# A hybrid decoder layer: the first operands of the feed-forward's down stage are read back inside the last slab, the slab order is swapped, and two products share one PSUM bank

## The chip, the core and the metric

The kernel runs on one core of a Trainium2 chip. TensorE (PE) multiplies out of SBUF into eight PSUM banks; VectorE (DVE), ScalarE (ACT) and GpSimd (POOL) do the elementwise work; SyncE (SP) issues nearly all DMAs, in order, from one queue. The metric is the device time of one execution in microseconds (us): the median of three runs of the kernel before is 1153.75 us (1151.14 to 1154.53).

## The reference

One layer over 1024 prompt tokens and 8 sequences of 4 sample tokens, 1056 tokens in all, at model width 1024 and feed-forward width 2816, in float32. The change touches the second half of it:

```python
    mix = jnp.concatenate([a, m], axis=-1) @ w_out
    x = x + _rms(mix, n_mix_post)
    f = _rms(x, n_ffn_pre)
    f = (jax.nn.silu(f @ w_gate) * (f @ w_up)) @ w_down
    x = x + _rms(f, n_ffn_post)
    x = x + jax.nn.sigmoid(x @ w_ple_gate) * (p @ w_ple)
```

`_rms` is a root-mean-square norm over the 1024 channels. What comes before it (the input projection, windowed attention with sinks, the pooling mixer) is left as it was.

## The kernel before

**Number format.** Every float32 operand is split into a high part `h` and a low part `l` (a cast on ACT, L167, then a subtraction on DVE, L168), and each product is three matmuls, hh, hl and lh, accumulated in one bank. All matmuls are issued by line L126, so PE's rows in the profile are told apart by their operands: `fh`/`fl` are feed-forward inputs, `wh`/`wl` weights, `sh`/`sl` sums of weights, `hid` the hidden activations, `qh`/`ql` quarters of the down weights and `xo` hidden operands read back from DRAM.

**Tiling.** The tokens form three groups of 352. The feed-forward has 22 pairs of column tiles (below: pairs c = 0 to 21), taken in 11 slabs of two. Group 2 is multiplied directly: 24 matmuls for the gate, 24 for the up projection, and 48 for the part of the down projection that belongs to a slab. Groups 0 and 1 together go through a Strassen-Winograd scheme: with two halves of the weights and the two groups as a 2x2 block matrix, seven products of 12 matmuls each replace eight. The products of a pair are P1 (operand B11), P2 (B21), S2, S3, P4 (T4), S1 and S4; S products take their weights from `w_sums` (L1096), which makes four sums of 128x512 on POOL (L1106) in place over the raw weights, and splits the results on ACT and DVE.

**The walk.** `WALK` lists (slab, groups) in order: first five slabs for group 2 alone (`FIRST2`: 2, 4, 6, 8, 10), then all eleven slabs, those of `FIRST2` with groups (0, 1) and the others with (0, 1, 2). The program therefore ends its walk with slab 10 for groups 0 and 1. A pair of (0, 1, 2) holds 7x12 + 48 = 132 matmuls; a pair of (0, 1) holds 84, and the first pair of a (0, 1) slab another 48, the group-2 down products (`downs`, L1337) of the slab before it. `gate_up` (L1122) takes the products of one pair in order; the order of the matmuls is the order of the program text. ACT copies P1 out of its bank (L1145), DVE adds P2 to the copy, and ACT applies Silu to the sum (L1152).

**Hidden operands.** `stage` (L1060) splits each of the seven hidden operands of a pair into an `st` tile and, when a set of two slabs is full, issues its store to DRAM (L1070, `xd<-st`). The last set, set 5, holds one slab alone. `down7` (L1234) runs the down stage of groups 0 and 1 in steps; `x_get` (L1222) issues the loads of a step's operands (`xo<-xd`). `q_sum` (L308, the POOL instruction in L316) makes sums of quarters of the down weights on POOL.

**Around them.** `turn` counts matmuls, and a `chain(steps, wait)` is a list of small steps (the norms of a group, `ple_steps`, L1309) that starts only when `wait` more matmuls were issued; the first of its matmuls takes `acc`, the sum of squares that DVE accumulates in L874. `need` (L318) prepares weights four items ahead. The order of ACT, DVE, POOL and SP instructions is chosen by a scheduler when the program is built; each engine then runs its list in order. The last stage (`ple_first`, `ple_rest`) repeats the scheme for the per-layer gate.

Of the kernel before, what the change touches and what calls it, by code (L numbers as in the profile page):

```python
# [10 lines left out]
F32 = mybir.dt.float32  # L11
F32R = mybir.dt.float32r
AF = mybir.ActivationFunctionType
ALU = mybir.AluOpType
# [47 lines left out]
def trunk_kernel(  # L62
# [43 lines left out]
    def nm(s):  # L106
        cnt[0] += 1
        return f"{s}{cnt[0]}"
# [113 lines left out]
    def direct_item(src, shape):  # L222
        return item("direct", add_plan(src, shape))

    WGU, WD = [], []
    for s, gs in WALK:
        pairs_of = []
        for i in range(SLAB):
            c = SLAB * s + i
            jg = direct_item(w_gu[c, 0], [P, KC, P])  # L230
            if 0 not in gs:
                ju = direct_item(w_gu[c, 1], [P, KC, P])
            if i == 0 and WD and 2 in WALK[len(WD) - 1][1]:
                last_s = WALK[len(WD) - 1][0]
                WD[-1] = [direct_item(w_dn[last_s, j], [P, SLAB, 512]) for j in range(2)]
            if 0 in gs:
# [4 lines left out]
        WD.append(None)  # L241


    SETS = [list(range(i, min(i + 2, NSLAB))) for i in range(0, NSLAB, 2)]
# [3 lines left out]
    STEPS = [(k, (0, 1)) for k in FIVE + TWO]  # L248
    STEPS += [(k, at) for at in ((2, 3), (4, 5)) for k in FIVE]
    STEPS += [(k, (2, 3, 4, 5)) for k in TWO]  # L250
    WDN = {}
    for k, at in STEPS:
        for e in at:
# [54 lines left out]
    def q_sum(k, e):  # L308

        out, a, b, op = {  # L310
            "S1": ("22", "21", "22", ALU.add),
            "S3": ("21", "11", "21", ALU.subtract),
            "S2": ("11", "22", "11", ALU.subtract),
            "S4": ("12", "12", "11", ALU.subtract),
        }[k]
        ge.tensor_tensor(q_load(out, e), q_load(a, e), q_load(b, e), op=op)  # L316

    def need(k, ahead=LOOK):  # L318

        for i in range(len(made), min(k + ahead + 1, len(ITEMS))):  # L320
            kind, js = ITEMS[i]
            if kind in ("direct", "home"):
                w_split(js[0], act_tile if kind == "home" else None)
                made[i] = pairs[js[0]]
            elif kind == "half":
                w_load(js[0])
                t = w_tile([P, KC, P], "w2")
                made[i] = t[:, 0:4, :], t[:, 4:8, :]
                split(*made[i], raws[js[0]][:, 4:8, :])
            elif kind == "quarter":  # L330
                made[i] = q_split(q_load(QUARTER[js[0]], js[1]))
                for n in {"P4": ("S1", "S3", "S2"), "P2": ("S4",)}.get(js[0], ()):
                    for e in js[2]:
                        q_sum(n, e)
            elif kind == "dsum":
                out = {"S1": "22", "S3": "21", "S2": "11", "S4": "12"}[js[0]]
                made[i] = q_split(q_load(out, js[1]))
            else:
                for j in js:
                    w_load(j)  # L340
                made[i] = w_sums(*(raws[j] for j in js))
            for kind, js in ITEMS[i + 1 : i + 3]:
                if kind not in ("quarter", "dsum"):
                    for j in js:
                        w_load(j)
            for kind, js in ITEMS[i + 1 : i + 7]:
                if kind in ("quarter", "dsum"):
                    q_loads(kind, js)
        return made[k]

    def gemm(ps, ops, start=True, stop=True):

        last = len(ops) - 1
        for i, (wh, wl, xh, xl) in enumerate(ops):
            mm(ps, wh, xh, start=start and i == 0, stop=False)
            mm(ps, wh, xl, start=False, stop=False)
            mm(ps, wl, xh, start=False, stop=stop and i == last)

    def ops8(w, xs):

# [699 lines left out]
    def stage(key, pair, src):  # L1060

        e = next(i for i, ps in enumerate(SETS) if pair in ps)
        i = SETS[e].index(pair)
        if (key, e) not in staged:
            staged[key, e] = act_tile([P, 2, 2, N], F32R, "st")
        t = staged[key, e]
        split(t[:, 0, i, :], t[:, 1, i, :], src)
        if i == len(SETS[e]) - 1:
            d = dpool.tile([P, 2, 2, N], F32, name=nm("xd"))
            nc.sync.dma_start(d[:, :, : i + 1], t[:, :, : i + 1].bitcast(F32))  # L1070
            spilled[key, e] = d

    evens = []

# [47 lines left out]
    def gate_up(items, pair, slot, gs, pending):  # L1122

        ig, iu, is_ = items
        n = N

        def product(w, x):
            ps = bank()
            gemm(ps[:, :n], ops4(w, x))
            turn(12)  # L1130
            return ps[:, :n]

        def direct(w):
            ps = bank()
            gemm(ps[:, :n], ops8(w, fs[2]))
            turn(24)
            return ps[:, :n]

        def add(out, a, ps):
            ve.tensor_tensor(out, a, ps, op=ALU.add)  # L1140

        wg = need(ig)
        if 0 in gs:
            p1 = tmp(n, "p1")
            se.copy(p1, product(quarter(wg, 0), f7["B11"]))  # L1145
# [7 lines left out]
        if pending and 0 in gs:  # L1153
# [4 lines left out]
        if 2 in gs:  # L1158
            if slot == 0:
                new_hid[0] = half(2, F32R, "hid")  # L1160
            hid_put(slot, sl)
        if pending and 0 not in gs:
            pending()
        if 0 not in gs:
            return
        if 2 not in gs:
            p4 = product(quarter(wu, 1), f7["T4"])
# [12 lines left out]
        add(p1, p1, product(s["S4"], f7["B22"]))  # L1180
        se.activation(p1, p1, AF.Silu)
        ve.tensor_tensor(u3, u3, p1, op=ALU.mult)
        pair_put(pair, slot, c21, u3)
# [222 lines left out]
    def ple_first(a):  # L1406

        wp, w = W1[a]
        need(wp)
        wg = need(w)  # L1410
        if not p1s:
            p1s.append(half(0, s="p1"))
        p1 = p1s[0][:, a // 2, :]
        se.copy(p1, product(quarter(wg, 0), e7["B11"]))
        c11 = tmp(N, "c11")
        ve.tensor_tensor(c11, p1, product(quarter(wg, 1), e7["B21"]), op=ALU.add)
        ple_end(c11, wp, a, 0)

    def ple_rest(a, b):
        wp, w, js = W2[a]  # L1420
# [37 lines left out]
    for a in (7, 5, 3, 1):  # L1458
        ple_first(a)
    for m in range(4):  # L1460
        embed_early(W1[1][0], m, 1)
    finish(list(chains))
    for a, b in PAIRS:
        ple_rest(a, b)
# [86 lines left out]
```

## Time and profile before

| | before |
|---|---|
| median of three runs | 1153.75 us |
| profiled execution | 1154.42 us |
| its span in the trace | 1152.6 us |
| VectorE busy | 858.1 us (74%), 1303 instructions |
| ScalarE busy | 508.9 us (44%), 919 instructions |
| GpSimd busy | 266.2 us (23%), 193 instructions |

The span is the stretch that the trace covers; 1.8 us of the execution lie outside it. The five slabs of group 2 alone, then the eleven others, fill the trace up to 840 us; the down stage of groups 0 and 1 starts at 866 us, and the per-layer stage fills the last 120 us. A row of a view names line, engine, operation and tiles, and gives starts and durations in us; a wait is put down to the producer that came last.

### The profile page before, as it was taken

Reading aid. Unit: us, or ns where it says so; the run is one execution under the profiler, and the core shown is the slowest. Engines: PE = TensorE matmul, PEld = TensorE weight load, DVE = VectorE, ACT = ScalarE, POOL = GpSimd, SP = SyncE. Lnnn points to the kernel's source line nnn. Section 1 sums busy time; section 2 is a strip of 40 time slices with the busy share of each in tenths; the row PEclk is TensorE's granted clock in tenths of the full one; section 3 lists DMA queues with packets and bytes.
Section 4 is the critical chain, followed back from the end, with each engine's and each line's share of the span. In section 5 each row is a group of like instructions: output and inputs, shape, how many; then the busy total and the mean of one; then the engine's idle time right before and its main releaser. Section 6 shows DMA issues by size and latency. Waiting matters only on the chain.

```text
span 1152.6 us, 17678 instructions
## 1 busy us (share of the span) xinstructions
PE 1092.3 (95%) x6867; PEld 1070.8 (93%) x6867; DVE 858.1 (74%) x1303; ACT 508.9 (44%) x919; POOL 266.2 (23%) x193
## 2 busy tenths in 40 slices
PE   8999999999999999999999999999819999789997
PEld 8999988899999999999999999999719999789996
DVE  6766379768979758686876976876875387898877
ACT  7322377645654333434433343433615522454442
POOL 0054022100000212232231321331251086000231
PEclk9999999999999999999999999999869999899998
DMA  7121311623633212532613523527539656725242
GB/s 280 55 68 55 99 48 38 243 87 113 244 128 129 74 44 67 188 134 79 225 59 122 199 73 107 188 82 274 191 107 406 235 192 213 269 69 188 101 128 76
DMA packets 54451, 163.60 MB, mean 142 GB/s; under 512 B 5828, under 2 KB 20068, under 8 KB 54368
## 3 DMA queue, kind: packets, MB, share of 16 engines
q1 hardware_dynamic: 53040, 160.70, 39.6%
q10 hardware_dynamic: 1328, 1.77, 0.5%
q8 instruction: 54, 0.88, 0.3%
q14 instruction: 29, 0.24, 0.1%
HBM read 124.59 MB, written 37.86 MB: 141 GB/s over the span
## 4 chain that ended last, share of the span: by engine, by line
PE 72%; DVE 11%; DMA 5%; ACT 4%; POOL 4%; issue 3%; POOLq 0%; SPq 0%; ACTq 0%; DVEq 0%
PE b L126 71%; POOL wr L1106 4%; DMA wr<-in_w_gu_dram 2%; DVE st L168 2%; DVE u L1270 2%; DVE wl L168 1%; ACT wh L167 1%; DVE ql L168 1%; DVE sl L168 1%; DMA xr<-in_x_dram 1%; ACT sh L167 1%; PE b L120 1%; DVE acc L874 1%; ACT h L454 1%; DMA xo<-xd 0%
## 5 line engine op out<-in xcount | busy, mean ns | idle before, releaser
L126 PE MATMUL b<-fh,wh 128*128 128x352 f32 x712 | 230.1, 323 | 0.3 <-DVE o L1202 0.3
L126 PE MATMUL b<-fh,wl 128*128 128x352 f32 x712 | 228.8, 321 | 0.0
L126 PE MATMUL b<-fl,wh 128*128 128x352 f32 x712 | 228.4, 321 | 0.0
L1106 POOL TENSOR_TENSOR wr<-wr 128x512 f32<-128x512 f32 x52 | 74.6, 1435 | 617.2 <-DVE wl L168 313.5
L167 ACT CAST wh<-wr 128x1024 fp32r<-128x1024 f32 (+1 forms) x125 | 128.3, 1028 | 192.0 <-PE b L126 122.4
L168 DVE TENSOR_TENSOR wl<-wr,wh 128x1024 fp32r<-128x1024 f32 (+1 forms) x125 | 153.1, 1227 | 35.3 <-ACT wh L167 34.7
L126 PE MATMUL b<-xo,qh 128*128 128x352 f32 x616 | 150.1, 327 | 25.5 <-DMA xo<-xd 25.5
L126 PE MATMUL b<-fh,sh 128*128 128x352 f32 x416 | 137.3, 330 | 8.2 <-ACT sh L167 5.8
L126 PE MATMUL b<-fh,sl 128*128 128x352 f32 x416 | 136.8, 329 | 3.2 <-DVE sl L168 3.2
L126 PE MATMUL b<-fl,sh 128*128 128x352 f32 x416 | 135.9, 327 | 0.0
L126 PEld LDWEIGHTS b<-fh,wh 128*128 128x128 f32 x712 | 133.7, 188 | 0.7 <-DVE o L1202 0.6
L126 PEld LDWEIGHTS b<-fl,wh 128*128 128x128 f32 x712 | 134.1, 188 | 0.0
L126 PEld LDWEIGHTS b<-fh,wl 128*128 128x128 f32 x712 | 133.8, 188 | 0.0
L126 PEld LDWEIGHTS b<-xo,qh 128*128 128x128 f32 x616 | 108.9, 192 | 25.8 <-issue 25.8
L168 DVE TENSOR_TENSOR sl<-wr,sh 128x1024 fp32r<-128x1024 f32 x52 | 63.5, 1221 | 68.1 <-ACT sh L167 67.7
L126 PE MATMUL b<-h,wh 128*128 128x352 f32 x480 | 105.8, 326 | 0.8 <-ACT h L454 0.8
L126 PE MATMUL b<-xo,ql 128*128 128x352 f32 x308 | 100.3, 326 | 0.2 <-DVE ql L168 0.2
L167 ACT CAST sh<-wr 128x1024 fp32r<-128x1024 f32 x52 | 53.9, 1043 | 101.7 <-POOL wr L1106 101.7
L126 PEld LDWEIGHTS b<-fh,sh 128*128 128x128 f32 x416 | 80.2, 193 | 9.9 <-ACT sh L167 7.3
L126 PE MATMUL b<-hid,wh 128*128 128x352 f32 x352 | 84.3, 322 | 1.6 <-DVE c L1140 1.6
L126 PEld LDWEIGHTS b<-fh,sl 128*128 128x128 f32 x416 | 80.2, 193 | 5.1 <-DVE sl L168 5.1
L168 DVE TENSOR_TENSOR ql<-wq,qh 128x1024 fp32r<-128x1024 f32 (+1 forms) x42 | 61.8, 1491 | 30.6 <-ACT qh L167 18.2
(204 smaller groups left out, 2189.4 us busy)
## 6 DMA issues: line engine op xcount, KB each, us to landing
wr<-in_w_gu_dram SPq DMA_DIRECT2D x64, 512.0 KB, 3.9
xd<-st SPq DMA_DIRECT2D x35, 704.0 KB, 4.9
xo<-xd SPq DMA_DIRECT2D x35, 704.0 KB, 6.0
wr<-in_w_dn_dram SPq DMA_DIRECT2D x22, 512.0 KB, 3.3
wq<-in_w_dn_dram SPq DMA_DIRECT2D x20, 512.0 KB, 6.5
wr<-in_w_pg_dram SPq DMA_DIRECT2D x18, 512.0 KB, 3.7
x<-in_x_dram SPq DMA_DIRECT2D x6, 704.0 KB, 9.1
x1d<-x SPq DMA_DIRECT2D x6, 704.0 KB, 3.6
```

The source lines that it names most:

```text
L120: ins = te.transpose(out, src, ident)
L126: ins = te.matmul(*args, **kw)
L167: fix(se.copy(hi, src))
L168: fix(ve.tensor_tensor(lo, src, hi.bitcast(F32), op=ALU.subtract))
L454: fix(se.activation(hi[:, c, :], t[:, c, :], AF.Identity, scale=gc))
L874: ve.tensor_tensor(acc_g, acc_g, sq, op=ALU.add)
L1106: ge.tensor_tensor(out, a, b, op=op)
L1270: ve.tensor_tensor(out, a, b, op=ALU.add)
```

## The change

**Slab order.** `FIRST2` becomes (1, 3, 5, 7, 9), so the last slab of the walk is one of (0, 1, 2). Its group-2 down products, 48 matmuls, come behind the walk.

**Operands and stores at the end of the walk.** `x_get(0)` and `x_get(1)`, called at the end of the walk and in `down7` before, are called ahead of the two pairs of the last slab. The seven stores of set 5 are issued by a new function `spill` after the last group-2 down products in program order.

**Down products shared.** `down_at` gives each pair of a (0, 1) slab one half of the 48 down products of the slab before; each pair of such a slab then holds 108 matmuls.

**P1 and P2 in one bank.** ACT copies P1 out as before; then P2's 12 matmuls accumulate onto the same bank (`onto`), so PE starts P2 only behind the copy, and Silu reads the bank. The DVE addition goes, 22 times in `gate_up` and 4 in the last stage (`ple_first`, which becomes a generator so that two of its column tiles interleave). In a (0, 1) slab P4 now stands between P1 and P2.

**The rest.** `q_sum` works slice by slice (20 more POOL instructions, each half as wide where a set has two slabs); the sums of sets 0 and 1 move in the program text from behind P4's to behind P2's quarters; the waits of the three `ple_steps` chains grow from 24 to 60, 64 and 56 matmuls. The matmuls are the same in number.

```diff
-    FIRST2 = tuple(range(NSLAB - 2 * AHEAD + 1, NSLAB, 2))
+    FIRST2 = tuple(range(NSLAB - 2 * AHEAD, NSLAB, 2))
...
-    LAST2 = max(n for n, (_, gs) in enumerate(WALK) if 2 in gs)
+    LAST2 = len(WALK) - 1
...
+    def down_at(n, i):
+        if not n or 2 not in WALK[n - 1][1]:
+            return ()
+        if 2 in WALK[n][1]:
+            return () if i else (0, 1)
+        return (i,)
...
-        ge.tensor_tensor(q_load(out, e), q_load(a, e), q_load(b, e), op=op)
+        for i in range(len(SETS[e])):
+            ge.tensor_tensor(*(q_load(q, e)[:, i, :] for q in (out, a, b)), op=op)
...
-    def gemm(ps, ops, start=True, stop=True):
+    def gemm(ps, ops, start=True, stop=True, onto=False):
         last = len(ops) - 1
+        kw = dict(skip_group_check=True) if onto else {}
+        start = start and not onto
...
-            d = dpool.tile([P, 2, 2, N], F32, name=nm("xd"))
-            nc.sync.dma_start(d[:, :, : i + 1], t[:, :, : i + 1].bitcast(F32))
-            spilled[key, e] = d
+            spilled[key, e] = dpool.tile([P, 2, 2, N], F32, name=nm("xd"))
+            if e < len(SETS) - 1:
+                spill(key, e)
+
+    def spill(key, e):
+        n = len(SETS[e])
+        nc.sync.dma_start(spilled[key, e][:, :, :n], staged[key, e][:, :, :n].bitcast(F32))
...
         if 0 in gs:
             p1 = tmp(n, "p1")
-            se.copy(p1, product(quarter(wg, 0), f7["B11"]))
+            ps1 = product(quarter(wg, 0), f7["B11"])
+            se.copy(p1, ps1[:, :n])
         if 2 in gs:
             sl = tmp(n, "sl")
             se.activation(sl, direct(wg), AF.Silu)
+        elif 0 in gs:
+            p4 = product(quarter(need(iu), 1), f7["T4"])
         if 0 in gs:
             c11 = tmp(n, "c11")
-            add(c11, p1, product(quarter(wg, 1), f7["B21"]))
-            se.activation(c11, c11, AF.Silu)
+            se.activation(c11, product(quarter(wg, 1), f7["B21"], ps1)[:, :n], AF.Silu)
...
-    def downs(n):
+    def downs(n, halves):
         hid[:] = old_hid
-        for m in range(KC):
-            down(n, m)
-            if n == LAST2:
-                finished(m, 2)
+        for h in halves:
+            for m in range(4 * h, 4 * h + 4):
+                down(n, m)
+                if n == LAST2:
+                    finished(m, 2)
...
         for i in range(SLAB):
-            first = i == 0 and n and 2 in WALK[n - 1][1]
-            gate_up(WGU[n][i], s, i, gs, (lambda: downs(n - 1)) if first else None)
-        if n == len(WALK) - 1:
-            x_get(0)
+            if n == len(WALK) - 1:
+                x_get(i)
+            gate_up(WGU[n][i], s, i, gs, lambda: downs(n - 1, down_at(n, i)))
+    old_hid = list(new_hid)
+    downs(LAST2, (0, 1))
+    for k in OPERAND.values():
+        spill(k, len(SETS) - 1)
     share[0] = 0.3
-    chain(ple_steps(2), 24)
+    chain(ple_steps(2), 60)
...
-    chain(ple_steps(0), 24)
+    chain(ple_steps(0), 64)
...
-    chain(ple_steps(1), 24)
+    chain(ple_steps(1), 56)
```

What this does to the engines' lists shows at three places. The rows name line, operation and tiles with the number of each tile; the change shifts the line numbers by 17 to 22 here.

**ACT, around the first pair of the first (0, 1) slab (pair 2).** `sh` is the cast of a weight sum that POOL made from this pair's weights, `p` on the left of a COPY the copy of P1, ACTIVATE `c` the Silu behind P2. Before:

```order
L167 CAST wh_4420<-wr_4271 128x1024
L1181 ACTIVATE p_4362<-p_4362 128x352
L167 CAST wh_4452<-wr_4360 128x1024
L167 CAST st_4537<-u_4472 128x352
L167 CAST st_4541<-c_4302 128x352
L1145 COPY p_4566<-b_4567 128x352
...
L167 CAST sh_4556<-wr_4190 128x1024
L1152 ACTIVATE c_4608<-c_4608 128x352
```

The same place in the changed kernel:

```order
L167 CAST wh_4414<-wr_4269 128x1024
L167 CAST sh_4452<-wr_4188 128x1024
L1199 ACTIVATE p_4358<-p_4358 128x352
L1167 COPY p_4562<-b_4563 128x352
L167 CAST st_4541<-u_4476 128x352
L167 CAST sh_4456<-wr_4234 128x1024
...
L1175 ACTIVATE c_4594<-b_4563 128x352
```

The copy of P1 stood ahead of the first cast of a weight sum and now stands behind it, and Silu reads P1's own bank, `b_4563`.

**SP, at the end of the walk.** `xd<-st` are the stores of hidden operands, `xo<-xd` the loads of the down stage; tiles of 256x1x352 belong to set 5. Before:

```order
L1070 DMA xd_8364<-st_8361 256x1x352
L295 DMA wq_8787<-in_w_dn_dram 128x2x512
...
L1070 DMA xd_8370<-st_8367 256x1x352
...
L1070 DMA xd_8523<-st_8520 256x1x352
L1231 DMA xo_8525<-xd_4825 128x1408
L1231 DMA xo_8527<-xd_5593 128x1408
L1231 DMA xo_8529<-xd_5026 128x1408
```

In the changed kernel:

```order
L1249 DMA xo_7964<-xd_4725 128x1408
L1092 DMA xd_7943<-st_7578 128x1408
L177 DMA wr_7836<-in_w_gu_dram 128x1024
...
L1249 DMA xo_7966<-xd_5485 128x1408
...
L1249 DMA xo_8172<-xd_4913 128x1408
L1249 DMA xo_8174<-xd_5673 128x1408
...
L1092 DMA xd_8166<-st_8163 256x1x352
...
L1092 DMA xd_8372<-st_8369 256x1x352
L1333 DMA pr_8583<-in_p_dram 128x352
L1249 DMA xo_8540<-xd_4899 128x1408
```

The loads of the first two steps' operands, four `xo` tiles, now stand ahead of all seven stores of set 5.

**PE, from the walk's end into the down stage.** `b<-fh,sl` are products of the walk, `hid` rows are group-2 down products, and the three matmuls of 128x1 with `acc` begin the norm of group 2 (`ple_steps(2)`). Before:

```order
L126 MATMUL b_8481<-fh_3969,sl_8272 128x352
L126 MATMUL b_8534<-xo_8525,qh_8294 128x352 x2
...
L126 MATMUL b_8548<-xo_8527,ql_8373 128x352
L126 MATMUL b_8574<-c_82,acc_8174 128x1 x3
L126 MATMUL b_8588<-xo_8525,qh_8294 128x352 x2
```

In the changed kernel:

```order
L126 MATMUL b_8334<-fl_3970,sh_8038 128x352
...
L126 MATMUL b_8464<-hid_8078,wl_8177 128x352
L126 MATMUL b_8484<-xo_7964,qh_8238 128x352 x2
...
L126 MATMUL b_8545<-xo_8174,ql_8425 128x352
L126 MATMUL b_8595<-c_82,acc_8385 128x1 x3
L126 MATMUL b_8609<-xo_8172,qh_8373 128x352 x2
```

48 matmuls with `hid` now lie between the last product of the walk and the first matmul of the down stage, and the norm's matmuls stand 60 matmuls behind that first one where they stood 24 behind it.

More of the change, by code (lines that the diff above doesn't have):

```diff
@@ L230, in trunk_kernel @@
             jg = direct_item(w_gu[c, 0], [P, KC, P])
-            if 0 not in gs:
+            if gs != (0, 1, 2):
                 ju = direct_item(w_gu[c, 1], [P, KC, P])
[L233 to L236, printed above, removed]
+            for j in down_at(n, i):
+                WD[n - 1].append(direct_item(w_dn[WALK[n - 1][0], j], [P, SLAB, 512]))
+            if gs == (0, 1, 2):
                 ju = direct_item(w_gu[c, 1], [P, KC, P])
@@ L240, in trunk_kernel @@
         WGU.append(pairs_of)
-        WD.append(None)
+        WD.append([])
+    WD[-1] = [direct_item(w_dn[WALK[-1][0], j], [P, SLAB, 512]) for j in range(2)]
     SETS = [list(range(i, min(i + 2, NSLAB))) for i in range(0, NSLAB, 2)]
@@ L250, in trunk_kernel @@
     STEPS += [(k, (2, 3, 4, 5)) for k in TWO]
+    SUMS_AT = ["P2", "P2"] + ["P4"] * 4
     WDN = {}
@@ L349, in need @@
         return made[k]
-    def gemm(ps, ops, start=True, stop=True):
+    def gemm(ps, ops, start=True, stop=True, onto=False):
         last = len(ops) - 1
+        kw = dict(skip_group_check=True) if onto else {}
+        start = start and not onto
         for i, (wh, wl, xh, xl) in enumerate(ops):
-            mm(ps, wh, xh, start=start and i == 0, stop=False)
-            mm(ps, wh, xl, start=False, stop=False)
-            mm(ps, wl, xh, start=False, stop=stop and i == last)
+            mm(ps, wh, xh, start=start and i == 0, stop=False, **kw)
+            mm(ps, wh, xl, start=False, stop=False, **kw)
+            mm(ps, wl, xh, start=False, stop=stop and i == last, **kw)
     def ops8(w, xs):
@@ L1125, in gate_up, with product @@
         n = N
-        def product(w, x):
-            ps = bank()
-            gemm(ps[:, :n], ops4(w, x))
+        def product(w, x, onto=None):
+            ps = bank() if onto is None else onto
+            gemm(ps[:, :n], ops4(w, x), onto=onto is not None)
             turn(12)
-            return ps[:, :n]
+            return ps
         def direct(w):
@@ L1139, in add @@
         def add(out, a, ps):
-            ve.tensor_tensor(out, a, ps, op=ALU.add)
+            ve.tensor_tensor(out, a, ps[:, :n], op=ALU.add)
         wg = need(ig)
@@ L1161, in gate_up @@
             hid_put(slot, sl)
-        if pending and 0 not in gs:
+        if 0 not in gs:
             pending()
-        if 0 not in gs:
             return
-        if 2 not in gs:
-            p4 = product(quarter(wu, 1), f7["T4"])
         s = need(is_)
@@ L1412, in ple_first @@
             p1s.append(half(0, s="p1"))
[L1413 to L1417, printed above, removed]
+        ps = bank()
+        gemm(ps[:, :N], ops4(quarter(wg, 0), e7["B11"]))
+        turn(12)
+        se.copy(p1s[0][:, a // 2, :], ps[:, :N])
+        yield
+        gemm(ps[:, :N], ops4(quarter(wg, 1), e7["B21"]), onto=True)
+        turn(12)
+        ple_end(ps[:, :N], wp, a, 0)
     def ple_rest(a, b):
@@ L1457, in trunk_kernel @@
     finish(chains[:-1])
[L1458 to L1461, printed above, removed]
+    firsts = [ple_first(a) for a in (7, 5, 3, 1)]
+    next(firsts[0])
+    for a, b in zip(firsts, firsts[1:] + [()]):
+        list(zip(range(1), b))
+        if not b:
+            for m in range(4):
+                embed_early(W1[1][0], m, 1)
+        list(a)
     finish(list(chains))
```

12 lines of the change are left out of this document (7 added, 5 removed).

## The prediction, made before the changed kernel was run

> **What bounds the kernel now.** I read the page first: which engine fills the span, how the clock runs, and where the chain that ended last goes.
>
> ```profile
> span 1152.6 us, 17678 instructions
> PE 1092.3 (95%) x6867; PEld 1070.8 (93%) x6867; DVE 858.1 (74%) x1303; ACT 508.9 (44%) x919; POOL 266.2 (23%) x193
> PEclk9999999999999999999999999999869999899998
> PE 72%; DVE 11%; DMA 5%; ACT 4%; POOL 4%; issue 3%; POOLq 0%; SPq 0%; ACTq 0%; DVEq 0%
> ```
>
> PE is busy 95% of the span and carries 72% of the chain. The change keeps every matmul, so it can only win time in which PE stands still or runs at a reduced clock. The clock row dips at slices 29, 30 and 35. PE's own waits say for whom it stood still:
>
> ```profile
> PE b L126 <- DMA xo<-xd: 25.5, 1, 25.5
> PE b L126 <- DVE acc L874: 11.8, 3, 7.4
> PE b L126 <- ACT sh L167: 5.8, 5, 3.3
> PE b L126 <- DVE sl L168: 3.2, 6, 0.7
> ```
>
> To price a stall with its loss of clock I use busy time by stage (columns: window, length, then for PE, PEld, DVE, ACT and POOL the busy time and count, then granted clock, DMA share, GB/s).
>
> ```profile
> 500.00:580.00 80.00, 79.03 (x495) 78.36 (x495) 61.69 (x91) 31.34 (x49) 22.18 (x17) 1.00 0.36 130
> 580.00:590.00 10.00, 8.69 (x53) 8.11 (x53) 6.77 (x11) 4.17 (x6) 5.44 (x4) 1.00 0.10 24
> 660.00:674.00 14.00, 12.00 (x64) 11.41 (x63) 10.21 (x15) 6.14 (x9) 5.57 (x5) 0.88 0.26 77
> 674.00:740.00 66.00, 66.00 (x415) 66.00 (x414) 50.10 (x75) 24.84 (x39) 16.75 (x13) 1.00 0.40 141
> 740.00:750.00 10.00, 9.07 (x55) 8.49 (x54) 6.80 (x11) 4.94 (x8) 4.61 (x4) 1.00 0.16 53
> 800.00:840.20 40.20, 34.74 (x196) 33.42 (x194) 33.63 (x50) 22.07 (x38) 11.26 (x8) 0.92 0.56 202
> 840.20:870.00 29.80, 4.27 (x16) 3.98 (x16) 18.72 (x11) 3.45 (x7) 15.79 (x6) 0.54 0.43 159
> 990.00:1006.50 16.50, 9.12 (x44) 8.83 (x43) 13.32 (x29) 6.67 (x14) 0.00 (x0) 0.69 0.77 292
> 1030.00:1040.50 10.50, 6.83 (x30) 6.54 (x29) 10.40 (x17) 7.03 (x12) 0.00 (x0) 0.67 0.71 228
> ```
>
> The stretch 674 to 740 is undisturbed: 66.00 us / 415 = 0.159 us per matmul. What a window holds beyond its count times 0.159 is lost there. Walk: 1.3 (500 to 580), 1.6, 3.8, 1.3 and 9.0 (800 to 840), together **17.0**. From 840.2 to 870, the reload: **27.3**. At 990, the norm of group 0: **9.5**. At 1030, the norm of group 1: **5.7**. Sum 59.5 us. Some matmul records may be missing, which makes a loss look larger by 0.16 each.
>
> **Part 1, the reload (removes 27.3).** POOL, DVE and SP from the last product at 840.2 on:
>
> ```profile
> 841.23 15.95 POOL L316 TENSOR_TENSOR wq<-wq,wq 128x1024 f32<-128x1024 f32 x6 [12.99 <-DVE ql L168]
> 844.58 2.66 DVE L1182 TENSOR_TENSOR u<-u,p 128x352 f32<-128x352 f32 x1
> 858.99 0.52 DVE L168 TENSOR_TENSOR st<-u,st 128x352 fp32r<-128x352 f32 x1
> 840.05 20.23 SPq L1070 DMA_DIRECT2D xd<-st  x5
> 860.37 2.29 SPq L1231 DMA_DIRECT2D xo<-xd  x4
> ```
>
> Six sums on POOL take 15.95 us. Beside them a DVE addition of two SBUF tiles takes 2.66 us, against 0.52 once POOL is done. So the last splits end at 859.5, SP holds the stores until then, and the loads behind them leave at 860.4 and are waited for until 866.0. In the changed queue the loads of two steps stand ahead of the seven stores, and 48 matmuls (7.6 us) run before the first of them is needed. I take the DMA wait as gone.
>
> What is late next is DVE. The same sums now start near the end of those 48 matmuls, as twelve half-width ones. The first matmul of the down stage needs a bank that DVE frees with an addition into `o`, which stands behind the last splits: I put 1.9 us for about one held split and two additions. Then the norm of group 2 needs six `acc` additions of two SBUF tiles each:
>
> ```profile
> 804.96 2.98 POOL L1106 TENSOR_TENSOR wr<-wr,wr 128x512 f32<-128x512 f32 x2
> 805.19 1.62 DVE L1078 TENSOR_TENSOR c<-c,c 128x352 f32<-128x352 f32 x1
> L874 DVE TENSOR_TENSOR acc<-acc,sq 128x352 f32<-128x352 f32 x42 | 21.6, 518 | 8.3 <-ACT sq L873 8.0
> ```
>
> In step with half-width sums such an addition takes 1.6 us instead of 0.52. Six of them, a held split of a weight quarter (2.3 us, estimated from one POOL instruction and a half) and the PSUM additions between (some 2 us) make about 14; PE has 60 matmuls, 9.6 us, until its three `acc` matmuls, so it waits 4.4. Bounds: 0, if POOL's sums come after the additions, to 14 if all of DVE's work there is held as in the rows above. With a half-clock stretch (2.5 us, as 9.5 at 990 is 7.4 of waiting and 2.1 of clock) this part costs **8.8**, bounds 0 to 20.
>
> **Part 2, the walk's waits (removes 17.0).** The chain from a weight's arrival to its sums, at pair 1, and the POOL work between:
>
> ```profile
> wr<-in_w_gu_dram SPq DMA_DIRECT2D x64, 512.0 KB, 3.9
> 407.07 1.05 ACT L167 CAST wh<-wr 128x1024 fp32r<-128x1024 f32 x1 [4.56 <-PE b L126]
> 409.54 1.30 POOL L1106 TENSOR_TENSOR wr<-wr 128x512 f32<-128x512 f32 x1 [16.08 <-DVE wl L168]
> 413.82 1.29 POOL L1106 TENSOR_TENSOR wr<-wr 128x512 f32<-128x512 f32 x1
> 415.14 1.05 ACT L167 CAST sh<-wr 128x1024 fp32r<-128x1024 f32 x1 [6.35 <-POOL wr L1106]
> 416.09 0.49 ACT L1181 ACTIVATE p<-p 128x352 f32<-128x352 f32 x1
> 416.49 1.04 ACT L167 CAST sh<-wr 128x1024 fp32r<-128x1024 f32 x1
> 417.43 0.45 ACT L1145 COPY p<-b 128x352 f32<-128x352 f32 x1
> 416.52 0.32 PE L126 MATMUL b<-fh,wh 128*128 128x352 f32 x1
> ```
>
> From the cast at 407.07 to the end of the second sum's cast at 417.53 are 10.5 us; with 3.9 for the load, one round takes 14.4 us before raw buffers come free, or 15 to 16 behind DVE's split. A second pair of a (0, 1) slab holds 84 matmuls, 13.4 us: PE outruns the round, and each such slab stalls. With 108 matmuls, 17.2 us, it doesn't. So all 17.0 go, bounds 13 to 17 since the last stretch also holds a wait of 2 us for a bank that could return.
>
> **Part 3, P1 and P2 in one bank (adds waits).** Before, P2 had a bank of its own. In the rows above the copy of P1 ends at 417.88, behind `sh`, Silu and `sh`, while P2's first matmul started at 416.52. In the changed kernel P2 must wait for the copy: 417.88 - 416.52 = **1.4 us**, for the six second pairs of (0, 1, 2) slabs: 8.4 us. At the first pair of each of the five (0, 1) slabs the copy stands behind `sh` and a Silu in ACT's list, and `sh` behind POOL's sums of that pair's weights, whose cast begins when P4 of the pair before frees a buffer. From that cast to the end of `sh` were 9.1 us (407.07 to 416.19); with 0.4 for Silu and 0.45 for the copy it is 10.0, and 10.8 where POOL is held by DVE. PE meanwhile has S1, S4, P1 and P4, 48 matmuls, 7.6 us. P2 waits 2.4 to 3.2 us; I take 2.7, 13.5 for five. Queued behind the waiting matmul is all of PE; at the other eleven pairs I estimate from the same rows that the copy ends 1.5 us or more before P2's turn, since no cast of a sum stands ahead of it then.
>
> Does such a wait also cost clock? At 580 two gaps lost 1.6 us and the clock stayed at 1.00; at 660 the gaps were these, and it fell to 0.88, which is 1.7 us of the 14:
>
> ```profile
> 664.49 0.32 PE L126 MATMUL b<-fh,wl 128*128 128x352 f32 x1
> 666.15 0.43 PE L126 MATMUL b<-fh,sh 128*128 128x352 f32 x1 [1.34 <-ACT sh L167]
> 667.41 0.43 PE L126 MATMUL b<-fh,sl 128*128 128x352 f32 x1 [0.67 <-DVE sl L168]
> 668.56 0.50 PE L126 MATMUL b<-fh,sl 128*128 128x352 f32 x1
> ```
>
> Gaps of 1.4 therefore cost no clock, gaps of 2.4 to 3.2 probably 1.7 each in three of five: 5.1. Part 3 together: 8.4 + 13.5 + 5.1 = **27.0**. Bounds: 0, if ACT runs the copies early, to 11 x (3.2 + 1.7) = 54.
>
> The Trainium skill, in "TensorE: Matmul & The Clock Gate", section "HAM oscillation — how this bites in real kernels", gives as its abstract rule that no idle gap of PE be longer than about 3.4 us. By that rule these waits, and the 4.4 at the norm perhaps aside, would cost no clock at all. The rows at 664 speak against it: two gaps, 1.3 and 0.7 us of waiting within 3 us, were enough.
>
> What goes in this part, 26 DVE additions of 0.51 us, was beside PE's work and is worth nothing.
>
> **Part 4, the later norms (remove 15.2).** `acc` was waited for 7.4 us at 993; its matmuls now stand 42 later, 6.7 us, which leaves 0.8. At 1031 they stand 36 later, 5.7 us, against a wait of about 3.8: nothing is left. Of 9.5 + 5.7 the change wins **14.4**, bounds 8 (the adds slip with the matmuls) to 15.2.
>
> **Part 5, costed at nothing.** The 20 added POOL instructions do the same elements, beside PE; without that cover a sum is 1.5 us. The two halves of the last stage's products keep 12 matmuls between copy and P2 by interleaving; if not, four waits of 0.5 to 2 us. ACT's list has two table loads more, beside the norm of group 1:
>
> ```profile
> L383 ACT ACT_TABLE_LOAD x4 | 5.1, 1283 | 0.1
> ```
>
> One is 1.3 us on an engine that is busy 44%, beside some 50 us of PE's products for group 2; with that cover gone they cost 2.6.
>
> **Sum.** 1154.4 - 27.3 + 8.8 - 17.0 + 27.0 - 14.4 = **1131.5**, from the profiled execution of 1154.42 us, which lies 0.7 above the median of the runs shown. I predict **1131**.
>
> **The rivals.** (a) **The P2 waits don't show**, because ACT reaches its copies in time: 1131.5 - 27.0 = 1104.5. For it speaks that ACT is busy only 44%; against it, the row at 417.43, a copy that ran 4.4 us after P1's last matmul. (b) **The waits come without the clock**, which is the page's rule as a mechanism here: 5.1 + 2.5 less, 1124. The row at 668.56 speaks against it. (c) **The end of the walk still waits**: the held DVE chain, or a store ahead of a load in SP's queue, keeps 15 us more of the 27.3: 1146. For it speaks that the same POOL sums still run there; against it, that no load stands behind the last splits any more. (d) **Slower**: the copy behind the weight sums at L1145 stalls P2 at 16 of 22 pairs, each with a half-clock stretch: 2.7 + 1.7 = 4.4, 70 instead of 27.0, 1175. It decides from an average of (27.0 + 22.9) / 22 = 2.3 us a pair; my sum has 1.2. That the change doesn't do what it says, with the operands late in spite of their place, is (c).
>
> **How the numbers follow.** A measurement of this kernel can tell about 0.3%, 3.5 us, from no change. Forecast 0.54, (a) 0.13, (b) 0.11, (c) 0.14, (d) 0.08. Faster: the first three and most of (c), 0.88; (c)'s upper end, within 0.3%, 0.04; slower 0.08. The range reaches to (a) and (c): 1103 to 1147 leaves out (d) and a part of (c)'s upper side. The forecast's own range is 1122 to 1140.
>
> **What would show it.** PE waiting for ACT `p` at L1167 11 times, 22 us; no wait for `xo`; a wait for `acc` near the start of the down stage; no wait for `sh` or `sl` in the walk; the clock at 1.00 in the second pairs. Without waits for `p`, part 3 is wrong; with waits at nearly every pair, (d).

## The result, and the profile after

The changed kernel takes 1135.45 us (median of 4 executions, 1129.69 to 1136.01) against 1152.51 us before: a ratio of 0.9843, 95% interval 0.9811 to 0.9875. 1131 was predicted, with 1103 to 1147 as the range. The profiled execution is the fastest of them, 1129.69 us, so its trace shows some 6 us less than a usual execution; the first experiment below says where these lie.

The page's head and the clock row of the changed kernel, and then PE's waits in it (total us, times, longest):

```profile
span 1127.9 us, 17622 instructions
PE 1085.8 (96%) x6867; PEld 1063.7 (94%) x6867; DVE 826.8 (73%) x1277; ACT 510.2 (45%) x921; POOL 276.9 (25%) x213
PEclk9999999999999999999999999999999999999999
```

```profile
PE b L126 <- ACT p L1167: 22.0, 11, 3.0
PE b L126 <- DVE acc L891: 5.3, 3, 3.9
PE b L126 <- DVE dg L414: 3.3, 3, 1.7
PE b L126 <- DVE p L1449: 1.7, 1, 1.7
```

The wait for `xo` (25.5 us) and those for `sh` and `sl` (9.0 together) are gone, and the wait for `acc` fell from 11.8 to 5.3. In their place PE waits 11 times for ACT's copy of P1, 22.0 us. Busy time by stage, read as in the prediction with 0.159 us a matmul:

```profile
800.00:855.00 55.00, 53.50 (x332) 52.96 (x331) 35.08 (x57) 23.60 (x39) 10.27 (x8) 1.00 0.74 266
855.00:880.00 25.00, 19.33 (x112) 18.76 (x111) 24.69 (x24) 15.12 (x29) 21.86 (x14) 0.93 0.74 294
985.00:996.00 11.00, 10.36 (x66) 9.94 (x65) 10.90 (x22) 7.67 (x14) 0.00 (x0) 1.00 0.89 352
```

From the walk's end into the down stage PE runs on at full clock. The norm of group 2 then costs 25.00 - 112 x 0.159 = 7.2 us, the norm of group 0 0.5 us.

One of the new waits, at the first pair of a (0, 1) slab, on PE, ACT and POOL:

```profile
520.05 0.32 PE L126 MATMUL b<-fh,wl 128*128 128x352 f32 x1
523.39 0.43 PE L126 MATMUL b<-fh,wh 128*128 128x352 f32 x1 [3.02 <-ACT p L1167]
521.55 1.04 ACT L167 CAST sh<-wr 128x1024 fp32r<-128x1024 f32 x1 [5.93 <-POOL wr L1127]
522.50 0.49 ACT L1199 ACTIVATE p<-p 128x352 f32<-128x352 f32 x1
522.90 0.43 ACT L1167 COPY p<-b 128x352 f32<-128x352 f32 x1
520.26 1.26 POOL L1127 TENSOR_TENSOR wr<-wr 128x512 f32<-128x512 f32 x1
```

POOL's last sum ends at 521.52, then come `sh`, Silu and the copy in ACT's order, and P2 starts when the copy ends at 523.33. ACT had stood idle for 5.93 us before `sh` with the copy behind it in its list.

### The profile page after: what moved, and what is told of

It is laid out like the page before. It is cut to its first block, busy times and chain, and to the rows that moved or that the text cites. A ratio compares the mean times of both kernels' runs of the same rounds, so it can differ in the third digit from the quotient of the medians.

```text
span 1127.9 us, 17622 instructions
## 1 busy us (share of the span) xinstructions
PE 1085.8 (96%) x6867; PEld 1063.7 (94%) x6867; DVE 826.8 (73%) x1277; ACT 510.2 (45%) x921; POOL 276.9 (25%) x213
## 5 line engine op out<-in xcount | busy, mean ns | idle before, releaser
L126 PE MATMUL b<-fh,wh 128*128 128x352 f32 x712 | 232.2, 326 | 22.3 <-ACT p L1167 22.0
L168 DVE TENSOR_TENSOR wl<-wr,wh 128x1024 fp32r<-128x1024 f32 (+1 forms) x125 | 161.2, 1292 | 34.5 <-ACT wh L167 33.9
L126 PE MATMUL b<-fh,sh 128*128 128x352 f32 x416 | 134.4, 323 | 2.1 <-DVE p L1449 1.7
L126 PE MATMUL b<-fh,sl 128*128 128x352 f32 x416 | 134.0, 322 | 0.0
L126 PE MATMUL b<-fl,sh 128*128 128x352 f32 x416 | 133.5, 321 | 0.0
L327 POOL TENSOR_TENSOR wq<-wq,wq 128x512 f32<-128x512 f32 x44 | 71.9, 1673 | 75.5 <-DVE ql L168 64.3
L126 PEld LDWEIGHTS b<-h,wh 128*128 128x128 f32 x480 | 82.4, 190 | 2.0 <-ACT h L471 1.4
```

What stands on the lines that cost most here:

```text
L126: ins = te.matmul(*args, **kw)
L168: fix(ve.tensor_tensor(lo, src, hi.bitcast(F32), op=ALU.subtract))
L327: ge.tensor_tensor(*(q_load(q, e)[:, i, :] for q in (out, a, b)), op=op)
```

## The experiments

### The same kernel again: what differs between executions

> The changed kernel once more, unaltered. Its profiled execution took 1129.7 us at a mean granted clock of 0.996, its other executions 1135.3 to 1136.3 at 0.984 to 0.987. Theory 1: the waits of PE for the copy of P1 are the same in all of them (22 us), and the difference is the clock alone: the waits of about 3.0 us at the first pairs of the last four (0, 1) slabs lie 81.84 us apart, which is 23.98 stretches of 3.413 us, so in one execution all four meet the grid of these stretches at the same place and either all cost a half-clock stretch (4 x 1.65 = 6.6 us) or none. Then executions lie near 1130 or near 1136 and hardly between, and a profile at 1136 shows the same waits and a clock below 1.00 right behind each of the four. Rival 1: a wait itself differs between executions (a DMA that is late); then a profile at 1136 shows a longer or a further wait.

Measured: 1134.39 us (1133.80 to 1134.49, 4 executions); the profiled one, 1134.49, waits 22.3 us for `p` in 11 times, the longest 3.0. The times lie between the 1130 and the 1136 of theory 1, where it expected hardly any. The five first pairs of (0, 1) slabs, in stretches of 12 us, first in the profile of the changed kernel above, then in this one:

```profile
436.00:448.00 12.00, 9.07 (x48) 8.78 (x47) 8.42 (x15) 6.12 (x11) 2.36 (x2) 0.86 0.35 117
519.00:531.00 12.00, 8.98 (x56) 8.70 (x55) 8.37 (x16) 6.84 (x11) 2.44 (x2) 1.00 0.36 125
...
683.00:695.00 12.00, 8.98 (x57) 8.70 (x56) 8.65 (x15) 6.84 (x11) 2.12 (x2) 1.00 0.34 119
764.00:776.00 12.00, 8.98 (x56) 8.70 (x56) 8.37 (x14) 6.84 (x11) 2.88 (x3) 1.00 0.40 131
```

```profile
437.00:449.00 12.00, 9.06 (x47) 8.77 (x46) 8.60 (x15) 6.16 (x11) 2.18 (x2) 0.86 0.33 113
520.00:532.00 12.00, 8.98 (x39) 8.69 (x38) 8.04 (x14) 5.84 (x10) 2.13 (x2) 0.72 0.29 107
604.00:616.00 12.00, 9.06 (x47) 8.77 (x46) 8.58 (x15) 6.13 (x11) 2.20 (x2) 0.86 0.32 113
687.00:699.00 12.00, 8.98 (x48) 8.70 (x48) 8.62 (x15) 6.39 (x11) 2.16 (x2) 0.86 0.31 115
770.00:782.00 12.00, 9.06 (x57) 8.77 (x56) 9.01 (x16) 6.84 (x11) 1.77 (x2) 1.00 0.27 100
```

The waits are the same; the clock is not. In the first profile one of five waits cost clock, in the second four. So rival 1 falls. That all of the last four go together is half right: none of them lost clock in the first profile, three of four did in the second. The clock records of the traces change in stretches of 3.41 us, at full or at half clock; the first profile has a half-clock one from 439.94 to 443.35, which fixes the grid. A lost stretch moves the next wait against it. In the first profile the wait from 437.37 to 440.30 had 2.57 us in the stretch ahead of the half-clock one; the wait from 520.37 to 523.39 lay across two stretches, about half in each, and no clock was lost.

The Trainium skill, in "TensorE: Matmul & The Clock Gate", section "HAM oscillation — how this bites in real kernels", has no idle gap above about 3.4 us as its rule. Here waits of 3.0 us lost clock in four of five cases of one execution, so the measurement decides: a shorter wait is enough.

### P2 in its own bank

```diff
-            se.activation(c11, product(quarter(wg, 1), f7["B21"], ps1)[:, :n], AF.Silu)
+            add(c11, p1, product(quarter(wg, 1), f7["B21"]))
+            se.activation(c11, c11, AF.Silu)
```

> The changed kernel with P2 in a bank of its own in the walk and the addition of P1 and P2 back on DVE (22 times); order of the products as in the changed kernel. Theory 1 (the shared bank makes PE wait for ACT's copy, and these waits also set off the half-clock stretches): the 11 waits for p, 22 us, go, and with them the clock losses of the walk (8 us in a slow-clock execution, 1.7 in the profiled one); the additions hide beside PE: about 1107 in every execution, clock about 0.998. Rival 2 (the copy is late because ACT or DVE can't keep up, so that a wait comes back in another form, for Silu's result or for a bank): 1115 to 1130, with new waits of PE for DVE c or for c11. Rival 3 (what is won here is lost again since the weights' sums are the next to be late, a round of about 14.4 us against 108 matmuls, 17.2 us): waits for sh or sl return.

Measured: 1103.99 us (ratio to before 0.9584, 0.9571 to 0.9597), 30.4 us less than the changed kernel in the same set of runs (1134.39). At the first pair of the first (0, 1) slab the copy runs as late as ever, and PE works through it:

```profile
437.15 1.05 ACT L167 CAST sh<-wr 128x1024 fp32r<-128x1024 f32 x1 [5.96 <-POOL wr L1127]
438.50 0.43 ACT L1167 COPY p<-b 128x352 f32<-128x352 f32 x1
```

```profile
640.00:740.00 100.00, 99.76 (x624) 99.47 (x624) 72.11 (x110) 39.28 (x61) 28.57 (x21) 1.00 0.31 114
```

In 100 us of the walk PE is busy for 99.76 at full clock. The 22 additions on DVE, 11 us of work, cost next to nothing: a wait of rival 2's kind came, but a small one, 1.4 us in five times.

```profile
PE b L126 <- DVE c L1161: 1.4, 5, 0.3
```

The 30.4 us are the 22.3 us of waiting and about 8 of clock: theory 1 holds, and rivals 2 and 3 fall.

### The bank kept, more matmuls between P1 and P2

```diff
         if 0 in gs:
-            c11 = tmp(n, "c11")
-            se.activation(c11, product(quarter(wg, 1), f7["B21"], ps1)[:, :n], AF.Silu)
             pending()
         wu = need(iu)
...
             hid_put(slot, sl)
+        if 0 in gs:
+            c11 = tmp(n, "c11")
+            se.activation(c11, product(quarter(wg, 1), f7["B21"], ps1)[:, :n], AF.Silu)
```

> The changed kernel with the shared bank kept, but more matmuls between P1 and P2: in (0, 1) slabs the 24 down products, in (0, 1, 2) slabs the 24 of the direct up projection, stand ahead of P2 instead of behind it. Theory 1: 24 matmuls are 3.8 us, more than any of the 11 waits (1.4 to 3.0), so all 11 go and the time is about 1107, as with banks of their own. Rival 4: the copy moves back with the matmuls (it waits for something that PE frees after the down products), and the waits stay near 3 us: 1125 to 1136.

Measured: 1111.62 us (0.9656, 0.9643 to 0.9669). No wait for `p` is left, so the cover works, but five others are new:

```profile
PE b L126 <- DVE wl L168: 8.5, 5, 1.7
```

The down products now come 12 matmuls earlier, and their weights' low parts are not ready. Theory 1 was right on the waits and missed this price: 8.5 us, enough for the 7.6 us between this kernel and the one with banks of their own.

### The copy on DVE

```diff
-            se.copy(p1, ps1[:, :n])
+            ve.tensor_copy(p1, ps1[:, :n])
```

> The changed kernel with the copy of P1 made by DVE instead of ACT; shared bank and order kept. Theory 1 (the copy is late only by its place behind the cast of a weight sum in ACT's list): DVE takes it sooner, PE's waits for p fall to less than half of 22 us, time 1110 to 1122. Rival 5 (a copy between P1 and P2 is late on any engine, as DVE is busy 73% and stands behind splits that wait for ACT): waits stay at 15 us or more, 1122 to 1136.

Measured: 1167.22 us, slower than before (1.013, 1.0115 to 1.0144).

```profile
PE b L126 <- DVE p L1167: 43.4, 17, 4.4
```

PE now waits at 17 pairs, 43.4 us, with more half-clock stretches. Rival 5 holds, and more strongly than it was put (the time lies above its 1136). At one such pair DVE's list has the copy behind the split `sl`, which waits for ACT's `sh`:

```profile
531.04 1.23 DVE L168 TENSOR_TENSOR sl<-wr,sh 128x1024 fp32r<-128x1024 f32 x1 [3.60 <-ACT sh L167]
532.62 0.52 DVE L1167 COPY p<-b 128x352 f32<-128x352 f32 x1
```

A shared bank hands PE to whichever list the copy stands in. This is what rival (d) of the prediction feared, waits at nearly every pair, on another engine.

### All 48 down products at the first pair

```diff
-        if 2 in WALK[n][1]:
-            return () if i else (0, 1)
-        return (i,)
+        return () if i else (0, 1)
```

> The kernel with P2 in its own bank (1104.0 us), and the 48 down products again all at the first pair of a (0, 1) slab, so that its second pair holds 84 matmuls, 13.4 us. Theory 1 (a second pair of 84 matmuls outruns the round of loading a weight and making its sums, 14.4 to 16 us): PE's waits for sh and sl return at the five second pairs, 1 to 3 us each, partly with a half-clock stretch: 1110 to 1121. Rival 6 (those waits went because the up weights are asked for ahead of the down weights and P4 comes earlier, not because of the number of matmuls): within 2 us of 1104.

Measured: 1104.49 us (1103.60 to 1105.18), the same as with the halves shared. No wait for `sh` or `sl` came back. Theory 1 fell here: with the new slab order and P4 ahead, a second pair of 84 matmuls is enough, so the 108 weren't needed.

### P4 behind P2 again, with shared and with unshared down products

```diff
-            if gs != (0, 1, 2):
+            if 0 not in gs:
                 ju = direct_item(w_gu[c, 1], [P, KC, P])
...
-        elif 0 in gs:
-            p4 = product(quarter(need(iu), 1), f7["T4"])
...
+        if 2 not in gs:
+            p4 = product(quarter(wu, 1), f7["T4"])
         s = need(is_)
```

> The kernel with P2 in its own bank (1104.0 us), and in (0, 1) slabs the up weight again asked for behind the down weights and P4 again behind P2 and the down products, as in the kernel before; each pair keeps its 24 down products (108 matmuls). Sharing alone. Theory 1 (108 matmuls, 17.2 us, are enough for a round of 14.4 to 16): no waits for sh or sl, 1103 to 1106. Theory 1b (what counts is the early asking and P4's place, since putting 48 down products at the first pair changed nothing): waits for sh and sl return at the five second pairs, 1110 to 1122.

> The same as the run with P4 behind, and also all 48 down products at the first pair, so that the (0, 1) slabs are walked as in the kernel before. Theory 1 and 1b both expect the waits of before for sh and sl, about 15 to 17 us with the clock: 1115 to 1122. If they stay away, neither the number of matmuls nor P4's place removed them, and the slab order or the scheduler's lists did (rival 9): 1103 to 1107.

Measured: 1111.16 us with the halves shared (1109.35 to 1115.47; the profiled execution is the slowest), and 1101.81 us (1101.00 to 1103.56) with 48 at the first pair. Sharing alone, with P4 behind, brings waits, as theory 1b expected and against theory 1:

```profile
PE b L126 <- ACT sh L167: 4.6, 6, 1.0
PE b L126 <- DVE sl L168: 4.0, 6, 0.7
```

But the second kernel walks its (0, 1) slabs as the kernel before did, 84 matmuls at the second pair, and the waits stay away but for 1.0 us in two for `sl`. It differs from before in this stretch by the slab order alone, apart from the per-pair lists that the scheduler made of it: rival 9. The traces say how. ACT's weight casts ahead of a second pair's sums, and SP's queue, in the kernel before (its slab 6):

```profile
650.50 1.04 ACT L167 CAST wh<-wr 128x1024 fp32r<-128x1024 f32 x1
656.84 1.05 ACT L167 CAST wh<-wr 128x1024 fp32r<-128x1024 f32 x1 [5.30 <-DMA wr<-in_w_gu_dram]
639.24 10.15 SPq L1070 DMA_DIRECT2D xd<-st  x5
```

The same place in this kernel (its slab 7), and SP's queue:

```profile
674.45 1.05 ACT L167 CAST wh<-wr 128x1024 fp32r<-128x1024 f32 x1
678.25 1.06 ACT L167 CAST wh<-wr 128x1024 fp32r<-128x1024 f32 x1 [2.74 <-DMA wr<-in_w_gu_dram]
660.70 15.65 SPq L177 DMA_DIRECT2D wr<-in_w_gu_dram  x4
685.60 0.33 SPq L1090 DMA_DIRECT2D xd<-st  x1
```

A set of hidden operands is complete after an odd slab, and its stores, 704 KB each, go out in the slab behind it. Before, that was an even slab, one of (0, 1): five stores leave within 10 us just ahead of the second pair's weights, and ACT waits 5.30 us for the load. With the orders swapped the stores fall into a (0, 1, 2) slab, whose pairs hold 132 matmuls, and the wait is 2.74. The 2.6 us taken from a round of some 15 us are about what a second pair of 84 matmuls, 13.4 us, lacked; this is argued from the two traces. The loads' slowing is shown; that the five stores are its only cause is read from their place in the queue, and no run moved the stores alone.

It doesn't reach the largest of the five waits either, that of the last slab (3.3 us, in the stretch that was priced at 9.0 of the 17.0 us). There the load had landed at 817.5, and the cast came later, behind group 2's steps on `o` and `sq` in ACT's list:

```profile
819.62 0.59 ACT L1217 ACTIVATE o<-o,c 128x352 f32<-128x352 f32 x1
820.12 1.04 ACT L167 CAST wh<-wr 128x1024 fp32r<-128x1024 f32 x1
```

A matmul let go of the cast's buffer at 820.11, so which of the two held it isn't separated. With the swapped order these steps come behind the walk.

Why sharing with P4 behind is worse than not sharing stays open; the halves of the down weights are then asked for between a pair's own weights.

### The slab order of before, operands asked for early

```diff
-    FIRST2 = tuple(range(NSLAB - 2 * AHEAD, NSLAB, 2))
+    FIRST2 = tuple(range(NSLAB - 2 * AHEAD + 1, NSLAB, 2))
...
-    downs(LAST2, (0, 1))
```

`LAST2` and the last slab's down weights follow.

> The kernel with P2 in its own bank (1104.0 us), and the slab order of the kernel before: the last slab is one of (0, 1), so no group-2 down products lie behind the walk; the first two steps' operands are still asked for inside the last slab. Early asking alone, without the 48 matmuls of cover (the run with late asking kept the cover alone). Theory 2 (either part removes most of the 25.5 us, but with early asking alone the third step's operands, behind the seven stores in SP's list, are late: stores end some 20 us after the walk, loads take 6, two steps last 15.3): no wait for xo at the first matmul, one of 3 to 11 us at the third step, less the 7 us of the norm of group 2, whose sum of squares is ready early here: 1101 to 1110. Rival 10 (both parts are needed): a wait for xo of 15 us or more, 1115 to 1130.

Measured: 1113.14 us (1112.53 to 1114.76), above theory 2's range and just below rival 10's. The first matmul of the down stage doesn't wait. The third step does, behind the stores:

```profile
855.85 0.93 PE L126 MATMUL b<-xo,qh 128*128 128x352 f32 x2 [5.30 <-DMA xo<-xd]
839.89 11.14 SPq L1091 DMA_DIRECT2D xd<-st  x5
851.12 1.05 SPq L1249 DMA_DIRECT2D xo<-xd  x2
```

Its mechanism is theory 2's: 5.30 us at the third step, with the loads issued at 851.1 behind five stores. What theory 2 left out is a wait of 2.34 us for a copy into `u` just ahead of it, and small waits in the walk, 3.2 us in five for `wl` and 1.0 for a `wh`: with the old order the walk is tight again even with P4 ahead. But no wait for `sh` or `sl` is among them. So in the old order the halves, with P4 ahead, do remove the waits that they were made for, and the new order removes them without the halves; which of P4's place and the 108 matmuls does it in the old order, no run separates.

### The operands asked for late, cover kept

```diff
-            if n == len(WALK) - 1:
-                x_get(i)
...
         spill(k, len(SETS) - 1)
+    x_get(0)
```

> The kernel with P2 in its own bank (1104.0 us), and the first operands of the down stage asked for behind the last group-2 down products in program order instead of inside the last slab. In SP's list their loads then stand behind at least four of the seven stores of set 5. Theory 1 (the loads' place in the queue behind stores that wait for DVE cost the 25.5 us, and the 48 matmuls alone cover only 7.6 of it): PE waits for xo 10 to 18 us, less the 7 us that the norm's wait and its clock cost now: 1108 to 1118. Rival 7 (the 48 matmuls alone are enough cover): within 3 us of 1104.

Measured: 1104.09 us (1103.50 to 1104.26): no change. Rival 7's time, but not its reason:

```profile
PE b L126 <- DMA xo<-xd: 6.0, 2, 3.1
PE b L126 <- DVE acc L891: 1.4, 2, 0.7
```

PE does wait for the operands, 6.0 us, and in return the wait of 3.9 us for group 2's `acc` is gone. One wait has taken the place of another: asking early is worth nothing as long as the norm of group 2 is late anyway. The 48 matmuls cover 7.6 of the 25.5 us before. Most of the rest went another way:

```profile
824.88 18.56 POOL L327 TENSOR_TENSOR wq<-wq,wq 128x512 f32<-128x512 f32 x12 [22.66 <-DVE ql L168]
825.27 1.19 SPq L1092 DMA_DIRECT2D xd<-st  x2
826.52 4.12 SPq L1250 DMA_DIRECT2D xo<-xd  x5
```

POOL's sums start 6.5 us behind the walk's last product (818.4), where they started 0.7 behind it before, and DVE's last splits, 0.52 us each, are done at 825.7, some 7 us behind that product and not 19. So the stores, and the loads behind them, leave that much earlier. The sums wait for a split `ql` of DVE; that they wait longer here comes with the order that the scheduler chose, and no run changed it alone.

### The norms at 24 matmuls, and the norm of group 2 at 96

```diff
-    chain(ple_steps(2), 60)
+    chain(ple_steps(2), 24)
...
-    chain(ple_steps(0), 64)
+    chain(ple_steps(0), 24)
...
-    chain(ple_steps(1), 56)
+    chain(ple_steps(1), 24)
```

> The kernel with P2 in its own bank (1104.0 us), and the waits of the three norms' chains back to 24 matmuls. Theory 1 (the sums of squares are ready at a time set by DVE, and a later place only lets PE work meanwhile): the matmuls with acc stand 36, 42 and 36 earlier, so PE waits for acc about 5.7 + 6.7 + 4 us more, with 2 to 6 us of clock: 1120 to 1127. Rival 8 (the additions move with the matmuls in DVE's list): at most 5 us more.

Measured: 1122.62 us, 18.6 more than with its base (1103.99).

```profile
PE b L126 <- DVE acc L891: 21.3, 4, 9.5
```

21.3 us instead of 5.3: theory 1 holds, the sum of squares comes when DVE has it. With 96 for group 2 and the others as changed:

> The kernel with P2 in its own bank (1104.0 us), and the chain of the norm of group 2 waiting 96 matmuls instead of 60. Theory 1: the 36 matmuls, 5.7 us, cover the remaining wait for acc of 3.9 us, and the half-clock stretch behind it (3.1 us in the profile) goes too: 1097 to 1099. Rival 8 (the additions move with the matmuls): 1103 to 1105.

Measured: 1102.48 us (1100.71 to 1103.92), 1.5 us less, not 5 to 7.

```profile
PE b L126 <- DVE dg L414: 3.4, 2, 3.2
PE b L126 <- DVE acc L891: 1.4, 2, 0.8
```

The wait for `acc` went and one for `dg`, the next step of the same norm, came. Both theories were too simple: the additions didn't move, but the next step stands in the same DVE list, held beside POOL's sums: two splits `ql` ahead of it take 4.53 us, and one behind it takes 1.22.

### Both steps of the norm later

```diff
-    chain(ple_steps(2), 60)
+    chain(ple_steps(2), 96)
...
-        r = yield from rstd_steps(acc3[g], 28)
+        r = yield from rstd_steps(acc3[g], 64 if g == 2 else 28)
```

> The kernel with P2 in its own bank, the norm of group 2 waiting 96 matmuls, and the second part of that norm 64 matmuls behind the first instead of 28. With 96 alone (1102.5 us) the wait for acc of 3.9 us had gone, but PE stood 3.2 us for dg, the norm's next step, with a half-clock stretch behind it. Theory 1 (dg is late by DVE's queue, in which it stands behind held splits, and 36 more matmuls, 5.7 us, cover it): no wait for dg, 1097 to 1099. Rival 8 (a next step of the norm is late in its turn): 1101 to 1103.

Measured: 1096.22 us (1095.95 to 1096.82), a ratio to before of 0.9514 (0.9500 to 0.9528), and some 38 us less than the changed kernel's 1134.39. It is faster than the kernel before and than the changed kernel. Theory 1 holds: the wait for `dg` is down to 0.2 us, and the time lies just below its 1097. What PE still waits for in the second half is small:

```profile
PE b L126 <- DVE p L1450: 1.9, 1, 1.9
PE b L126 <- DVE acc L891: 1.4, 2, 0.7
```

## Why the prediction came out right, and where it did not

**The sum.** 1131 was forecast; 1129.69 is the profiled execution and 1135.45 the median. With the parts as the profiled execution has them, 1154.4 - 27.3 + 7.2 - 17.0 + 23.4 - 14.7, the sum is 1126.0; 3.7 us of it were not located. So some of the closeness is luck. By steps:

- **Part 1, the reload (27.3 removed, 8.8 added): right in size.** No wait for `xo` is left, and the norm of group 2 costs 7.2 us, 3.9 of it for `acc` against 4.4 forecast. The 1.9 us for a bank freed by DVE did not come; a wait for `dg`, not forecast, did. The reason was half right: with the stores ahead of the loads again PE waited only 6.0 us and the time stayed, so the early asking does nothing in this kernel. What does it is the 48 matmuls, 7.6 us, and splits that end some 12 us earlier after the walk, since POOL's sums start when they are nearly done; the prediction had these sums start late, but used that only for the norm.
- **Part 2, the walk's waits (17.0 removed): right in size, the cause at best one of two.** They went, but 108 matmuls against a round of 14.4 us are not the reason in this kernel. With 84 matmuls, P4 ahead or behind, they stay away; with 108 and P4 behind, some 7 us return (the 8.6 in the rows above hold one wait of each kind outside the walk). The step that failed is that a second pair of 84 matmuls must outrun the round: it took the load's 3.9 us and what stands around it as given. Before, ACT waited up to 5.30 us for the second pair's weights, just behind five stores, and the swapped slab order moved these into a slab with room. In the old order, 108 matmuls with P4 ahead also took the waits for `sh` and `sl` away, so the reason given would have served there. For the last slab, 9.0 of the 17.0, the cause stays open.
- **Part 3, the shared bank (27.0 added): right in place, count and size.** 11 waits of 22.0 us against 11 of 21.9. The six of 1.4 measured 1.2 on average, 7.1 us, and the five of 2.7 measured 3.0, 15.0 us: the two errors cancel, which is luck. The clock's share, 5.1, is 1.4 in the profiled execution (57 - 48 matmuls, in the first of the five stretches above) and up to 7.5 in another (10, 18, 10 and 9 matmuls lacking): this is the term that separates 1129.7 from the median.
- **Part 4, the later norms (14.4 won): right.** Group 0's norm costs 0.5 us where 0.8 was left over, and at group 1's norm no wait for `acc` is left. Put back to 24 matmuls, the three norms, group 2's with them, cost 18.6 us.

**The rivals.** (a), no P2 waits, is what an own bank makes of the kernel, and its time was 1104.5; the run took 1103.99. (b), waits without the clock, is what the profiled execution shows at four of its five waits of 3.0 us, and the median does not. (c) did not come. (d) did not come with the copy on ACT; waits at 17 pairs came with it on DVE, 1167.22 against 1175.

## What to carry to other kernels

A copy out of a PSUM bank that is to be accumulated on further puts the copying engine's whole list in front of TensorE; here it cost 22.0 us of waiting on ACT and 43.4 on DVE, and these waits went only with more matmuls between P1 and P2; the addition on DVE, with a bank of its own, cost 1.4. Price a change by its parts even when the sum comes out: two of the four gains here had, in whole or in part, another cause than the one that they were made for. Where a wait is removed, take away the next one in the same chain too: both steps of a norm together won 7.8 us, the first alone 1.5.

## What the runs showed of the hardware that was not expected

One and the same wait of 3.0 us cost no clock or up to 2.9 us (39 matmuls in a stretch instead of 57), by where it fell in the grid of 3.41 us stretches. Read against that grid in the two profiles, each of the five waits that cost clock had 2.4 us or more in one stretch, and each of the five that cost none had 1.8 at most. Where no clock is lost the waits return every 81.84 us (520.37, 602.22, 684.05 and 765.88 in the first profile), 23.98 stretches, and so meet the grid at nearly the same place until a lost stretch moves them. Executions of one kernel lay between 1129.7 and 1136.3 us, and the two that were profiled, 1129.69 and 1134.49, have the same waits in them.
